# One more empty side step ahead of two products in a hybrid decoder trunk

## The chip, the cores and the metric

The kernel runs on one core of a Trainium2 chip. The metric is the device time of one execution in microseconds; the median of three runs of the kernel before is 1079.74 us (1079.16 to 1080.49). TensorE (PE in the profile) multiplies matrices, with its weight loads listed as PEld; VectorE (DVE), ScalarE (ACT) and GpSimd (POOL) do elementwise work; SyncE (SP) issues most transfers.

## What is computed

The input is 256 positions of width 2048. There are two layers. Layer 0 projects the normed input to six parts of 1024 and runs two token mixers side by side: HGRN2, a gated linear recurrence with 8 heads of 128, and Griffin RG-LRU, a linear recurrence over channels. Layer 1 is an mLSTM. Both end in an output projection and a gated embedding.

```
# HGRN2 (per head, chunks of 64)
q = silu(q_pre);  f = lb + (1 - lb) * sigmoid(f_pre);  k = (1 - lb) * sigmoid(-f_pre)
S_t = diag(f_t) S_{t-1} + k_t v_t^T;   o_t = S_t^T q_t
# RG-LRU
xc = causal_conv(xb)                                   # 4 taps
r = sigmoid(xc @ w_r + b_r);  ig = sigmoid(xc @ w_i + b_i)      # blocks of 128
a = exp(-8 r softplus(-lam));  u = sqrt(1 - a^2) * ig * xc
h_t = a_t h_{t-1} + u_t
# both: * silu(gate), then one output projection
```

All data are float32.

## The kernel before, in words

**Weights.** Each weight tile of 128 x 1024 comes by SyncE's queue into one of five raw buffers. ScalarE casts it to a high half (whi, line 123), VectorE subtracts to get a low half (wlo, line 124); there are four buffers of each, so the two tiles of one step and the two of the next. TensorE multiplies high by high and low activations (line 155) and low by high (line 162).

**Blocks and quarters.** A block (lines 147 to 175) is one output tile of 128 features over all 256 positions: 16 matmuls with high weights, then 16 with low ones. For the gates the tokens are on the partitions instead (project_tok, lines 193 to 213): an output tile of 512 columns is made in four quarters, each of two halves of 12 matmuls (lines 208 to 210).

**Side work.** The mixers are Python generators in lanes. The function pump (line 75) takes one step, up to the next yield, of the first generator of each lane. It is called once in each block, between the high and the low matmuls, and once in each quarter, between its two halves. A generator that ends lets the next one of its lane take its first step in the same call. The text calls these calls slots and numbers them from the first block after attention group 0 is started:

- slots 1 to 4: forget gates f of group 1 (f_proj); 5 to 8: its queries q (q_proj)
- slots 9 to 12 and 13 to 16: the two halves of the RG-LRU's input (xb_proj), each of four blocks; each two blocks are followed by a convolution (conv), one pass on ScalarE (line 705) and three instructions on VectorE (line 708) for each of two tiles
- slots 17 to 20 and 21 to 24: the four quarters of the two output gates of HGRN2 (gate_tok)

Attention of a group (lines 524 to 617) is eight steps: the product qf = q * f; five levels (block lengths 1, 2, 4, 8, 16), in each of which TensorE makes small products of k and qf (lines 541 and 546) and VectorE then updates qf (line 553), k (line 554) and the running products tot (line 556), and copies into C (lines 558 and 562); the blocks off the diagonal ("banks", lines 605 and 610, copied by ScalarE in lines 594, 614 and 615); and the read-out (lines 636 and 639) with its copies and squares on ScalarE (lines 640 and 643) and a Newton reciprocal root on VectorE (lines 216 to 222, 644 to 650). A half of the RG-LRU (lines 662 to 697) is five steps: the load of its gate weights; two gate products (line 674) with their sigmoids (line 678); tanh and exponential (lines 684 and 685) with a product (line 686) and a square (lines 690 and 691); and the root (line 693), a product (line 694) and the scan (line 696).

**Order on the engines.** Within an engine instructions run in the order that a list scheduler wrote down; the casts and subtractions of weights have a high priority, and side work of a slot is kept behind the last weight instruction issued before it. PSUM has three banks for side products (mx), three for blocks (mm) and two more (st).

Of the kernel before, what the change touches and what calls it, by code (L numbers as in the profile page):

```python
# [44 lines left out]
def trunk(ctx: ExitStack, tc: tile.TileContext, a, out):  # L45
# [58 lines left out]
    def pc(name, i=0, n=None):  # L104
        o, w = PRM[name]
        return prm[:, o + i:o + i + (n or 1)]
# [379 lines left out]
    with m0_scope:  # L486
# [37 lines left out]
        def attention(g):  # L524
# [2 lines left out]
            Ac = m0.tile([P, 4, P], F32, name="Ac", tag="Ac", bufs=1)  # L527
            C = m0.tile([P, 8, 32], F32, name="C", tag="C", bufs=1)
            qf = m0.tile([P, 1024], F32, name="qf", tag="qf", bufs=1)
            v.tensor_tensor(out=qf, in0=q, in1=f, op=ALU.mult)  # L530
            if g == 0:
                gp.memset(A, 0.0)
# [129 lines left out]
        def rg_lru(r, xc):  # L662
            bw = m0.tile([P, 2, 512], F32, name="bw", tag="bw", bufs=1)
            sy.dma_start(out=bw, in_=a["bw"][r])
            av = m0.tile([P, 1024], F32, name="av", tag="f")
            tt = m0.tile([P, 1024], F32, name="tt", tag="k")
            it = m0.tile([P, 1024], F32, name="it", tag="it", bufs=1)
            yield
            for j in range(2):
                for w, (dst, bias) in enumerate(((av, "bbr"), (it, "bbi"))):  # L670
                    ps = px.tile([P, 512], F32, name="mx", tag="mx")
                    for i in range(2):
                        c = 2 * j + i
                        te.matmul(ps[:, i * T:(i + 1) * T], bw[:, w, c * P:(c + 1) * P], xc[:, c * T:(c + 1) * T],
                                  start=True, stop=True)
                    for i in range(2):
                        c = 2 * j + i
                        s.activation(dst[:, c * T:(c + 1) * T], ps[:, i * T:(i + 1) * T], AF.Sigmoid,
                                     bias=pc(bias, 4 * r + c))
                yield  # L680
            for c in range(4):
                b = 4 * r + c
                cc = slice(c * T, (c + 1) * T)
                s.activation(tt[:, cc], av[:, cc], AF.Tanh, scale=sp8[:, b:b + 1])
                s.activation(av[:, cc], av[:, cc], AF.Exp, scale=spm8[:, b:b + 1])
            v.tensor_tensor(out=it, in0=it, in1=xc, op=ALU.mult)
            for j in range(2):
                sq = tp.tile([P, 512], F32, name="sq", tag="sq")
                jj = slice(j * 512, (j + 1) * 512)
                s.activation(sq, av[:, jj], AF.Square)  # L690
                v.scalar_tensor_tensor(tt[:, jj], sq, 1.0, tt[:, jj], op0=ALU.add, op1=ALU.mult)
            yield
            s.activation(tt, tt, AF.Sqrt, scale=0.25)
            v.tensor_tensor(out=it, in0=it, in1=tt, op=ALU.mult)
            v.memset(av.rearrange("p (c t) -> p c t", t=T)[:, :, 0:1], 0.0)
            v.tensor_tensor_scan(tt, av, it, 0.0, op0=ALU.mult, op1=ALU.add)
            res["h", r] = tt
# [16 lines left out]
        f_proj(0)  # L714
        q_proj(0)
        start("att", attention(0))
        f_proj(1)
        q_proj(1)
        start("att", attention(1))
        start("rg", rg_lru(0, xb_proj(0)))  # L720
        start("rg", rg_lru(1, xb_proj(1)))
        y = {}
        held = {}
# [487 lines left out]
```

## Time and profile before

| | |
|---|---|
| median of three runs | 1079.74 us |
| profiled execution | 1078.11 us |
| span of its instructions | 1076.3 us |
| mean granted TensorE clock | 0.997 |
| busy share PE, DVE, ACT, POOL | 98%, 68%, 54%, 6% |

The page gives busy time by engine and the groups of instructions that cost most. The view of waits lists which instruction stood idle until which other one ended: microseconds in total, times, the longest. The view by stage gives for a stretch of time: its length, busy time (and count) of TensorE, of its weight loads, of VectorE, ScalarE and GpSimd, the granted clock, the share of the DMA engines and GB/s. The view in order of time gives start and duration in microseconds, and in brackets the idle time before an instruction with what ended it; "x64" is a run of 64 instructions whose duration is that of the whole run. In these counts one multiplication in float32 appears as several passes.

### The profile page before, as it was taken

Reading aid. Unit: us, or ns where it says so; the run is one execution under the profiler, and the core shown is the slowest. Engines: PE = TensorE matmul, PEld = TensorE weight load, DVE = VectorE, ACT = ScalarE, POOL = GpSimd, SP = SyncE. Lnnn points to the kernel's source line nnn. Section 1 sums busy time; section 2 is a strip of 40 time slices with the busy share of each in tenths; the row PEclk is TensorE's granted clock in tenths of the full one; section 3 lists DMA queues with packets and bytes.
Section 4 is the critical chain, followed back from the end, with each engine's and each line's share of the span. In section 5 each row is a group of like instructions: output and inputs, shape, how many; then the busy total and the mean of one; then the engine's idle time right before and its main releaser. Section 6 shows DMA issues by size and latency. Waiting matters only on the chain.

```text
span 1076.3 us, 16798 instructions
## 1 busy us (share of the span) xinstructions
PE 1055.6 (98%) x6500; PEld 910.4 (85%) x6500; DVE 735.1 (68%) x1106; ACT 584.8 (54%) x863; POOL 67.8 (6%) x72
## 2 busy tenths in 40 slices
PE   7999999999999999999999999999999999999996
PEld 6888888887888888888888888888888888888886
DVE  6868978877767557777544887855456677555665
ACT  7565455688654435556444666654445554434543
POOL 0140400000000000112000000000000000000111
PEclk9999999999999999999999999999999999999998
DMA  9667444445655555555654655545555755555552
GB/s 337 166 230 217 153 160 149 154 138 194 240 195 193 193 186 188 185 189 194 195 193 158 216 188 167 176 157 195 195 195 190 247 184 181 196 192 176 181 176 79
DMA packets 56576, 201.76 MB, mean 187 GB/s; under 512 B 6472, under 2 KB 6864, under 8 KB 56496
## 3 DMA queue, kind: packets, MB, share of 16 engines
q1 hardware_dynamic: 54720, 195.04, 54.1%
q0 software_dynamic: 1776, 5.65, 1.8%
q8 instruction: 51, 0.84, 0.3%
q14 instruction: 29, 0.24, 0.1%
HBM read 198.55 MB, written 2.11 MB: 186 GB/s over the span
## 4 chain that ended last, share of the span: by engine, by line
PE 93%; DVE 2%; ACT 2%; issue 1%; DMA 1%; SPq 0%; DVEq 0%; ACTq 0%
PE mm L155 31%; PE mm L162 16%; PE mm L208 12%; PE mm L209 12%; PE mm L210 12%; DVE wlo L124 1%; PE mm L1065 1%; PE mm L1064 1%; PE mm L1063 1%; PE nu L899 1%; PE mx L546 1%; DMA raw<-in_pw_dram 1%; PE mx L428 0%; ACT whi L123 0%; PE mm L143 0%
## 5 line engine op out<-in xcount | busy, mean ns | idle before, releaser
L124 DVE TENSOR_TENSOR wlo<-raw,whi 128x1024 fp32r<-128x1024 f32 (+1 forms) x361 | 444.9, 1255 | 257.9 <-ACT whi L123 145.7
L123 ACT CAST whi<-raw 128x1024 fp32r<-128x1024 f32 (+1 forms) x361 | 377.5, 1048 | 333.9 <-PE mm L155 163.4
L155 PE MATMUL mm<-ahl,whi 128*128 128x512 f32 x1536 | 367.8, 391 | 0.0
L155 PEld LDWEIGHTS mm<-ahl,whi 128*128 128x128 f32 x1536 | 282.0, 188 | 55.7 <-DVE ahl L139 0.6
L208 PE MATMUL mm<-whi,ahl 128*128 128x512 f32 x608 | 238.7, 393 | 0.0
L210 PE MATMUL mm<-whi,ahl 128*128 128x512 f32 x608 | 236.7, 389 | 0.0
L209 PE MATMUL mm<-wlo,ahl 128*128 128x512 f32 x608 | 236.7, 389 | 0.0
L162 PE MATMUL mm<-ahl,wlo 128*128 128x256 f32 x1536 | 201.8, 284 | 0.0
L162 PEld LDWEIGHTS mm<-ahl,wlo 128*128 128x128 f32 x1536 | 195.7, 191 | 6.2
L210 PEld LDWEIGHTS mm<-whi,ahl 128*128 128x128 f32 x608 | 114.1, 188 | 24.0
L208 PEld LDWEIGHTS mm<-whi,ahl 128*128 128x128 f32 x608 | 114.2, 188 | 23.3
L209 PEld LDWEIGHTS mm<-wlo,ahl 128*128 128x128 f32 x608 | 114.2, 188 | 23.0
L179 ACT COPY sm<-mm 128x256 f32<-128x256 f32 x64 | 23.7, 371 | 43.8 <-PE mm L162 43.8
L180 DVE TENSOR_TENSOR mg<-mm,sm 128x256 f32<-128x256 f32 x64 | 26.6, 416 | 0.8 <-ACT sm L179 0.7
L772 DVE SCALAR_TENSOR_TENSOR qk<-mg,prm,qk 128x255 f32<-128x255 f32 (+2 forms) x48 | 21.5, 480 | 5.7 <-ACT qk L769 5.5
L261 POOL TENSOR_TENSOR acc<-acc,sq 128x512 f32<-128x512 f32 x6 | 9.7, 1621 | 193.8 <-ACT sq L260 193.8
L1051 POOL TENSOR_TENSOR pl<-pl,row 128x512 f32<-128x512 f32 x6 | 9.2, 1527 | 191.3 <-ACT sq L1035 191.3
L1063 PE MATMUL mm<-whi,ahl 128*128 128x256 f32 x64 | 18.3, 285 | 0.0
L1065 PE MATMUL mm<-whi,ahl 128*128 128x256 f32 x64 | 18.1, 283 | 0.0
L1064 PE MATMUL mm<-wlo,ahl 128*128 128x256 f32 x64 | 18.1, 283 | 0.0
L190 DVE TENSOR_TENSOR mg<-mg,hrs 128x512 f32<-128x512 f32 (+1 forms) x25 | 17.8, 714 | 0.3
L143 PE MATMUL mm<-ahl,whi 128*128 128x256 f32 x32 | 10.0, 314 | 7.4 <-ACT whi L123 7.4
(293 smaller groups left out, 772.1 us busy)
## 6 DMA issues: line engine op xcount, KB each, us to landing
raw<-in_ew_dram SPq DMA_DIRECT2D x64, 512.0 KB, 5.0
raw<-in_g_dram SPq DMA_DIRECT2D x56, 512.0 KB, 4.1
raw<-in_eo_dram SPq DMA_DIRECT2D x32, 512.0 KB, 4.7
raw<-in_ov_dram SPq DMA_DIRECT2D x32, 512.0 KB, 4.8
raw<-in_oqk_dram SPq DMA_DIRECT2D x32, 512.0 KB, 4.6
raw<-in_oog_dram SPq DMA_DIRECT2D x32, 512.0 KB, 4.5
raw<-in_oz_dram SPq DMA_DIRECT2D x32, 512.0 KB, 4.3
raw<-in_oo_dram SPq DMA_DIRECT2D x32, 512.0 KB, 4.1
```

The lines of the kernel that those rows point to most:

```text
L123: last["act"] = s.copy(h, r).ins
L124: last["dve"] = v.tensor_tensor(out=l, in0=r, in1=h.bitcast(F32), op=ALU.subtract).ins
L155: last["pe"] = te.matmul(ps, parts[k // 8][0][:, c:c + P], act[k // 2][2][:, (k % 2) * 512:(k % 2 + 1) * 512], start=(k == 0), stop=False).ins
L162: last["pe"] = te.matmul(ps[:, T:2 * T], parts[k // 8][1][:, c:c + P], act[k // 2][0][:, k % 2], start=False, stop=(k == KT - 1)).ins
L179: s.copy(small, ps[:, T:2 * T])
L180: v.tensor_tensor(out=dst, in0=ps[:, 0:T], in1=small, op=ALU.add)
L208: te.matmul(ps[hf], xh, wh, start=(k == 0), stop=False)
L209: te.matmul(ps[hf], xh, wl, start=False, stop=False)
L210: last["pe"] = te.matmul(ps[hf], xl, wh, start=False, stop=(k == KT - 1)).ins
L1063: te.matmul(ps[hf], xh, wh, start=(k == 0), stop=False)
L1064: te.matmul(ps[hf], xh, wl, start=False, stop=False)
L1065: last["pe"] = te.matmul(ps[hf], xl, wh, start=False, stop=(k == KT - 1)).ins
```

## The change

One yield is added in attention, ahead of the product qf, and one in rg_lru, ahead of the loop of gate products.

```
@@ -527,6 +527,7 @@
             Ac = m0.tile([P, 4, P], F32, name="Ac", tag="Ac", bufs=1)
             C = m0.tile([P, 8, 32], F32, name="C", tag="C", bufs=1)
             qf = m0.tile([P, 1024], F32, name="qf", tag="qf", bufs=1)
+            yield
             v.tensor_tensor(out=qf, in0=q, in1=f, op=ALU.mult)
             if g == 0:
                 gp.memset(A, 0.0)
@@ -665,6 +666,7 @@
             av = m0.tile([P, 1024], F32, name="av", tag="f")
             tt = m0.tile([P, 1024], F32, name="tt", tag="k")
             it = m0.tile([P, 1024], F32, name="it", tag="it", bufs=1)
             yield
+            yield
             for j in range(2):
                 for w, (dst, bias) in enumerate(((av, "bbr"), (it, "bbi"))):
```

No operation is added or removed by it. The slots of the steps are these:

| step | before | with the change |
|---|---|---|
| group 0: qf / levels / banks / read-out | 1 / 2-6 / 7 / 8 | 2 / 3-7 / 8 / 9 |
| group 1: qf / levels / banks / read-out | 9 / 10-14 / 15 / 16 | 10 / 11-15 / 16 / 17 |
| half 0: load / two gate products / exponential / root and scan | 13 / 14, 15 / 16 / 17 | 13 / 15, 16 / 17 / 18 |
| half 1: load / two gate products / exponential / root and scan | 17 / 18, 19 / 20 / 21 | 18 / 20, 21 / 22 / 23 |

Group 1's empty step shares slot 9 with the read-out of group 0. Half 1 is shifted by two slots, once through half 0 ahead of it in the lane. From the RG-LRU's gates (gate_mul) on the order of the engines is the same as before. ScalarE has 16 table loads in place of 15, since a tanh of the first output gate now stands between the root of half 0 and the sigmoids of half 1.

VectorE around the product qf of group 0, in slots 1 and 2; q and mg are the last query tile, tot the product of neighbouring forget gates. Before:

```order
L124 TENSOR_TENSOR wlo<-raw,whi 128x1024 x2
L180 TENSOR_TENSOR mg<-mm,sm 128x256
L556 TENSOR_TENSOR tot_1332<-f 128x512
L190 TENSOR_TENSOR mg<-mg,hrs 128x512
L517 SCALAR_TENSOR_TENSOR q<-mg,omb,th 128x256 x2
L530 TENSOR_TENSOR qf<-q,f 128x1024
```

With the change:

```order
L180 TENSOR_TENSOR mg<-mm,sm 128x256
L190 TENSOR_TENSOR mg<-mg,hrs 128x512
L517 SCALAR_TENSOR_TENSOR q<-mg,omb,th 128x256 x2
L531 TENSOR_TENSOR qf<-q,f 128x1024
L124 TENSOR_TENSOR wlo<-raw,whi 128x1024 x2
L180 TENSOR_TENSOR mg<-mm,sm 128x256
L557 TENSOR_TENSOR tot_1386<-f 128x512
```

The product qf stays directly behind q; tot moves behind it and behind a pair of low halves. On TensorE the level-1 products move behind the next block's high matmuls.

VectorE at the end of the last convolution (xc of half 1), in slots 16 to 18. Before:

```order
L708 SCALAR_TENSOR_TENSOR xc<-mg,prm,xc 128x253
L708 SCALAR_TENSOR_TENSOR xc<-mg,prm,xc 128x254
L696 SCALAR_TENSOR_TENSOR tt<-av,it 128x1024
L124 TENSOR_TENSOR wlo<-raw,whi 128x1024 x2
L708 SCALAR_TENSOR_TENSOR xc<-mg,prm,xc 128x253
```

With the change:

```order
L710 SCALAR_TENSOR_TENSOR xc<-mg,prm,xc 128x253
L710 SCALAR_TENSOR_TENSOR xc<-mg,prm,xc 128x254
L710 SCALAR_TENSOR_TENSOR xc<-mg,prm,xc 128x253
L124 TENSOR_TENSOR wlo<-raw,whi 128x1024 x2
L645 TENSOR_SCALAR hss<-hss 128x8
```

The conv's last instruction stood behind the scan of half 0 and the low halves of quarter four; now all six stand in a row ahead of the low halves of quarter three, and the read-out of group 1 (hss) follows.

ScalarE at the casts for quarters three and four and the next tile, in slots 17 to 20. Before:

```order
L693 ACT_TABLE_LOAD
L693 ACTIVATE tt<-tt 128x1024
L123 CAST whi<-raw 128x1024 x2
L705 ACTIVATE xc<-mg,prm 128x256 x2
L678 ACT_TABLE_LOAD
L678 ACTIVATE av<-mx,prm 128x256 x2
```

With the change:

```order
L641 COPY o<-mx 128x512
L644 ACTIVATE sq,hss<-mx 128x128 x2
L123 CAST whi<-raw 128x1024
L644 ACTIVATE sq,hss<-mx 128x128
L123 CAST whi<-raw 128x1024
L644 ACTIVATE sq,hss<-mx 128x128
L692 ACTIVATE sq<-av 128x512 x2
L695 ACT_TABLE_LOAD
L695 ACTIVATE tt<-tt 128x1024
L123 CAST whi<-raw 128x1024 x4
L444 ACT_TABLE_LOAD
```

The two casts for quarter three stood behind the root of half 0; they now stand among the read-out's squares, ahead of that root, and the casts for quarter four and the next tile's first quarter behind it. From half 0's first gate sigmoid to the second of the casts for quarter three ScalarE's list has, with the change, 8 sigmoids, 4 tanh, 4 exponentials, 3 table loads, 2 copies of blocks, 4 casts, 4 + 7 copies of attention blocks, 2 conv passes, 2 copies and 7 squares of the read-out. VectorE's list between the low halves of quarters three and four is two products for the square (line 691), the Newton steps, the scaling of the read-out (line 650) and the product of line 694.

More of the change, by code (lines that the diff above doesn't have):

```diff
@@ L529, in attention @@
             qf = m0.tile([P, 1024], F32, name="qf", tag="qf", bufs=1)
+            yield
             v.tensor_tensor(out=qf, in0=q, in1=f, op=ALU.mult)
@@ L667, in rg_lru @@
             it = m0.tile([P, 1024], F32, name="it", tag="it", bufs=1)
+            yield
             yield
```

## The prediction

> **What bounds the kernel now.** I read the first part of the page, then TensorE's waits, then busy time by stage, then the instructions in order of time where TensorE waits.
>
> ```profile
> PE 1055.6 (98%) x6500; PEld 910.4 (85%) x6500; DVE 735.1 (68%) x1106; ACT 584.8 (54%) x863; POOL 67.8 (6%) x72
> ```
>
> TensorE is busy for 1055.6 of 1076.3 us. A change that adds or removes no matmul can only act on the 20.7 us that are left. The view of waits, for TensorE alone, tells which instructions they belong to:
>
> ```profile
> PE mm L143 <- ACT whi L123: 7.4, 2, 6.1
> PE mx L674 <- DVE xc L708: 2.3, 1, 2.3
> PE mx L546 <- DVE qf L530: 1.9, 1, 1.9
> ```
>
> The first is the start of the kernel, out of reach. The other two lie in the two generators that are edited: a gate product waits for the convolved tile xc, and a level-1 product waits for qf, each once. After them comes a long stage with no idle time at all:
>
> ```profile
> 400.00:1040.00 640.00, 640.00 (x3252) 546.34 (x3252) 414.12 (x564) 331.42 (x470) 28.96 (x32) 1.00 0.57 189
> ```
>
> Busy is 640.00 of 640.00 us at a granted clock of 1.00, and the order of the engines there is that of before. So what TensorE wins or loses ahead of it arrives at the end undiminished; no later wait can eat it.
>
> **The change, part 1: the wait for qf.** TensorE in order of time (start, duration, what; idle before it in brackets), first group 0, then the same step of group 1:
>
> ```profile
> 119.14 0.84 PE L541 MATMUL mx<-q,k 128*32 128x32 f32 x64
> 121.86 0.73 PE L546 MATMUL mx<-qf,k 128*32 128x16 f32 x64 [1.88 <-DVE qf L530]
> 122.53 2.17 PE L162 MATMUL mm<-ahl,wlo 128*128 128x256 f32 x16
> ...
> 176.09 0.73 PE L541 MATMUL mx<-q,k 128*32 128x32 f32 x62
> ...
> 177.31 2.18 PE L162 MATMUL mm<-ahl,wlo 128*128 128x256 f32 x16
> ```
>
> The step takes 122.53 - 119.14 = 3.39 us in group 0 and 177.31 - 176.09 = 1.22 us in group 1. The wait therefore costs 2.17 us, a little more than the 1.88 in brackets. VectorE shows why qf is late:
>
> ```profile
> 113.57 1.44 DVE L556 TENSOR_TENSOR tot<-f 128x512 f32<-128x512 f32 x1
> ...
> 119.63 2.18 DVE L530 TENSOR_TENSOR qf<-q,f 128x1024 f32<-128x1024 f32 x1
> ...
> 171.45 1.23 DVE L530 TENSOR_TENSOR qf<-q,f 128x1024 f32<-128x1024 f32 x1
> ```
>
> ```profile
> 107.44 13.28 POOL L332 TENSOR_TENSOR pl<-pl,plrs 128x512 f32<-128x512 f32 x8 [5.88 <-DMA plrs<-plrsd]
> ```
>
> In group 0 the product takes 2.18 us beside POOL's eight products of 107.44 to 120.72, in group 1, with POOL idle, 1.23 us. It ends at 121.81, and TensorE starts at 121.86. With the change qf still stands right behind q on VectorE, and tot (1.44 us) moves from ahead of it to behind it, so qf ends at about 120.4. TensorE asks for it one block later: an unburdened block is about 5.6 us (the same start of side work in two neighbouring blocks), so at 119.14 + 5.6 = 124.8. That leaves 4.4 us of room; were qf no earlier, 3.0. **Gain 2.17 us**, and nothing is likely to give it back: qf would have to be later than any row of this stage shows.
>
> **Part 2: the wait for xc.** TensorE at the two gate products of the second RG-LRU half (slots 18 and 19), and VectorE's end of the convolution:
>
> ```profile
> 233.21 1.89 PE L674 MATMUL mx<-xc,bw 128*128 128x256 f32 x8
> 234.74 0.58 PE L208 MATMUL mm<-whi,ahl 128*128 128x512 f32 x1
> ...
> 240.40 1.02 PE L674 MATMUL mx<-xc,bw 128*128 128x256 f32 x4
> 243.73 1.13 PE L674 MATMUL mx<-xc,bw 128*128 128x256 f32 x4 [2.31 <-DVE xc L708]
> 244.51 0.58 PE L208 MATMUL mm<-whi,ahl 128*128 128x512 f32 x1
> ```
>
> ```profile
> 238.75 2.28 DVE L696 TENSOR_TENSOR_SCAN tt<-av,it 128x1024 f32<-128x1024 f32 x1
> ...
> 243.20 0.47 DVE L708 SCALAR_TENSOR_TENSOR xc<-mg,prm,xc 128x253 f32<-128x253 f32 x1
> ```
>
> Undisturbed the step takes 234.74 - 233.21 = 1.53 us, delayed 244.51 - 240.40 = 4.11: it costs 2.58 us. The last of the conv's instructions stands behind the first half's scan and a pair of low halves, since that half's end shares slot 17. With the change the end of the first half moves to slot 18, and all six conv instructions stand ahead of the weight pair. Counted from the end of the last conv block, that is ScalarE's conv pass at some 5 us (its backlog of that stage) and six instructions of 0.40 on VectorE, 8 us in all; TensorE asks for the tile only after a read-out (2.60) and seven half quarters (2.73 each; rows of both in (b)), 21.7 us. **Gain 2.58 us.**
>
> **Part 3: what is late next.** Three places come close. (a) A level of group 1 beside the conv of the first half. VectorE has one block to update qf and k between two levels:
>
> ```profile
> 189.50 0.74 PE L546 MATMUL mx<-qf,k 128*32 128x16 f32 x64
> ```
>
> ```profile
> 188.17 0.68 DVE L554 TENSOR_TENSOR k<-k,tot 128x512 f32<-128x512 f32 x1
> ```
>
> The k update ends at 188.85, 0.65 us ahead of TensorE. The level before it stands at this place now, and one conv instruction more (0.40 from start to start) lies between the two updates: 0.25 us of room. VectorE's own start there depends on ScalarE's conv pass, so I allow 0 to 0.7 us of loss and take 0.2.
>
> (b) The fourth quarter of the first output gate. The read-out of group 1 moves from slot 16 into slot 17, and with it ScalarE's copies and squares, ahead of the casts of weights. ScalarE ran the same list before from the first gate sigmoid on, with no wait behind its first row:
>
> ```profile
> 203.02 1.99 PE L674 MATMUL mx<-xc,bw 128*128 128x256 f32 x8
> ...
> 216.78 3.82 PE L155 MATMUL mm<-ahl,whi 128*128 128x512 f32 x16
> 220.43 1.05 PE L636 MATMUL mx<-vt,A 128*128 128x128 f32 x8
> ...
> 223.03 2.15 PE L162 MATMUL mm<-ahl,wlo 128*128 128x256 f32 x16
> 225.01 0.40 PE L208 MATMUL mm<-whi,ahl 128*128 128x512 f32 x1
> ```
>
> ```profile
> 204.19 0.84 ACT L678 ACTIVATE av<-mx,prm 128x256 f32<-128x256 f32 x2 [0.64 <-PE mx L674]
> ...
> 208.08 1.28 ACT L685 ACT_TABLE_LOAD   x1
> 209.38 0.51 ACT L685 ACTIVATE av<-av,spm 128x256 f32<-128x256 f32 x1
> 209.79 1.03 ACT L123 CAST whi<-raw 128x1024 fp32r<-128x1024 f32 x1
> ...
> 226.44 0.56 ACT L684 ACTIVATE tt<-av,sp 128x256 f32<-128x256 f32 x1
> ```
>
> The list takes 226.44 - 204.19 = 22.25 us. The new one, up to the second cast for quarter three, has a tanh and an exponential more (0.41 each from start to start) and a square less (about 0.25): 22.8 us, from 1.17 us behind the gate product (204.19 - 203.02). VectorE then makes that low half (1.2), ends the first half's and the read-out's arithmetic and makes the next low half:
>
> ```profile
> 228.75 0.69 DVE L691 SCALAR_TENSOR_TENSOR tt<-sq,tt 128x512 f32<-128x512 f32 x1 [0.34 <-ACT sq L690]
> ...
> 230.49 0.16 DVE L221 TENSOR_TENSOR hnt<-hnt,hny 128x8 f32<-128x8 f32 x1
> ...
> 231.89 0.17 DVE L222 SCALAR_TENSOR_TENSOR hnr<-hnt,hnr 128x8 f32<-128x8 f32 x1
> 231.97 1.22 DVE L694 TENSOR_TENSOR it<-it,tt 128x1024 f32<-128x1024 f32 x1
> 233.11 2.35 DVE L124 TENSOR_TENSOR wlo<-raw,whi 128x1024 fp32r<-128x1024 f32 x2
> ```
>
> That is two products of 0.6, nine Newton steps of 0.20 (seven from 230.49 to 231.89), two large products of 1.14, small ones of 0.6: 5.9 us; then 1.2 for the half. In all 1.17 + 22.8 + 1.2 + 5.9 + 1.2 = 32.3 us. TensorE in the same time: gate product to the end of the block after it 13.76 (203.02 to 216.78), read-out 2.60 (220.43 to 223.03), and six half quarters at 2.73 (three in 225.01 to 233.21), 16.4: 32.8 us, and 0.2 more to the first matmul that takes the low half. Room 0.7 us, so no loss. If instructions don't overlap as well as before (some 40, 0.06 us each) it is late by 1.7 us. I take 0.1; the range is 0 to 1.7.
>
> (c) The second gate product of slot 16 takes the PSUM bank that ScalarE's first three copies (L614) free; the spacing of the two is as before, so I book nothing.
>
> The page called ScalarE: Activation LUTs of the Trainium skill (section What ACT_TABLE_LOAD costs) gives about 1.28 us for a table load plus 1.38 us of drain, 2.66 us for each switch. The change adds one load, and by that rule ScalarE's three switches in (b) would take some 4.1 us more, TensorE would lose 3.4 us there, and the sum would be a gain of only about 1.2 us. The trace disagrees: from a load to the instruction behind it are 1.30 us (208.08 to 209.38), so this gets no chance beyond that of the moved wait below.
>
> Sum: 2.17 + 2.58 - 0.2 - 0.1 = 4.4 us. Against the profiled execution's own 1078.11 us (span 1076.3) that gives 1073.7; the median of the runs shown, 1079.74, lies 1.63 higher, and I carry the difference over: **1075.3 us**.
>
> **The rivals.** *Part of it comes back.* Places (a) and (b) take their worst, 0.7 + 1.7 = 2.4 us; the gain is 2.3, the time 1077.4. For it: ScalarE is busy 27.02 of 30 us from 220 to 250. Against it: the list ran without gaps before.
>
> ```profile
> 220.00:250.00 30.00, 27.70 (x143) 23.53 (x142) 21.19 (x39) 27.02 (x54) 0.00 (x0) 1.00 0.40 128
> ```
>
> *The wait only moves.* An empty step doesn't shorten what VectorE and ScalarE must do; the wait for xc turns into one of equal size for a low half in quarters two to four, and only the gain for qf, 2.2 us, less the 0.2 of (a), is left: 1077.7, no change that can be told (0.2%, 2.2 us, is about what a measurement tells from none). For it: the read-out and the half's end now meet in slots 17 and 18. Against it: xc was late through its place in VectorE's queue, not by total work; VectorE is busy only 21.19 of those 30 us.
>
> *Slower.* The low half of quarter four comes as late as the chain of before would bring it. Before, from the end of the list (226.44) to the end of the low pair ahead of the last conv instruction (243.20) lie 16.8 us. If that chain does not shorten, the pair is there 1.17 + 22.8 + 16.8 = 40.8 us behind the gate product, and TensorE wants its second half 32.8 + 1.6 = 34.4 us behind it: 6.4 us late, and with the 0.7 of (a) the loss is 7.1, the time 1079.74 + 2.4 = 1082.1. It decides for slower once that pair is more than 6.2 us late. Against it: those 16.8 us hold the scan, the conv and another pair (2.28 + 2.9 + 2.35), which stand elsewhere now. The Trainium skill's page TensorE: Matmul & The Clock Gate (Part 1) would add to such a wait a halved clock after some 3.4 us of idling; no run here shows it, the stages around both waits having a granted clock of 1.00.
>
> **How the numbers follow.** Forecast 0.62, part comes back 0.18, wait moves 0.13, slower 0.07. The forecast and the second are faster by over 0.2% (under 1077.6): 0.79 after the second's tail; within: 0.14; slower: 0.07. From below the range is bounded by the full gain, 4.75, and half a microsecond of spread of the median (runs lie 0.6 to 0.75 around it): 1074.3. From above it takes in the part that comes back and most of the moved wait: 1078.0.
>
> **What would show it.** TensorE's waits have neither qf nor xc; the level-1 step of group 0 takes about 1.2 us as in group 1, both gate products of the second half 1.5. The low half for the fourth quarter is ready within a microsecond of its first use. Wrong would be: a wait for wlo, for k or for a PSUM bank of over 2 us between 180 and 260 us, or a stage behind 400 us that has lost its full TensorE.

## The result and the profile after

The changed kernel took 1073.82 us (median of 6 runs, 1072.39 to 1075.84), the kernel before 1079.55 us (6 runs, 1077.04 to 1080.88). The ratio is 0.9946, with a 95% interval of 0.9934 to 0.9958: faster by 5.7 us where 4.4 were forecast, and half a microsecond below the low end of the range. The profiled execution took 1074.66 us, its span is 1072.9. One execution of the changed kernel (1169.53 us at a mean granted clock of 0.851, the profiled one of e4 below) and one of the kernel before (6046.13 us) are far out of line and left out of all that follows.

First the busy time by engine of the changed kernel (line numbers are one higher than before from 530 on, two higher from 669 on), then TensorE's waits:

```profile
PE 1056.5 (98%) x6500; PEld 911.6 (85%) x6500; DVE 735.0 (69%) x1106; ACT 585.8 (55%) x864; POOL 68.4 (6%) x72
```

```profile
PE mm L143 <- ACT whi L123: 6.8, 2, 6.3
PE mx L547 <- DVE k L555: 0.4, 1, 0.4
```

TensorE's busy time is nearly what it was (1055.6 before). The waits for qf and for xc are gone. A wait of 0.4 us for k is new. In order of time, TensorE at the level-1 step of group 0, at the new wait, and at the gate products of the second RG-LRU half:

```profile
125.52 0.73 PE L542 MATMUL mx<-q,k 128*32 128x32 f32 x62
...
126.74 1.46 PE L162 MATMUL mm<-ahl,wlo 128*128 128x256 f32 x10
...
145.81 0.73 PE L547 MATMUL mx<-qf,k 128*32 128x16 f32 x64 [0.40 <-DVE k L555]
...
243.24 1.89 PE L676 MATMUL mx<-xc,bw 128*128 128x256 f32 x8
244.78 0.58 PE L208 MATMUL mm<-whi,ahl 128*128 128x512 f32 x1
```

The level-1 step takes 126.74 - 125.52 = 1.22 us (3.39 before), the gate products 244.78 - 243.24 = 1.54 (4.11 before). VectorE's product qf is as slow as before, beside GpSimd's products of 108.34 to 122.17 us, but it ends at 121.03, 4.5 us ahead of this step:

```profile
118.82 2.21 DVE L531 TENSOR_TENSOR qf<-q,f 128x1024 f32<-128x1024 f32 x1
```

VectorE also shows where the new wait comes from:

```profile
141.46 0.73 DVE L507 TENSOR_SCALAR f<-f,omb,lb 128x256 f32<-128x256 f32 x2 [1.22 <-ACT f L503]
142.11 0.69 DVE L554 TENSOR_TENSOR qf<-qf,tot 128x512 f32<-128x512 f32 x1
142.71 2.35 DVE L124 TENSOR_TENSOR wlo<-raw,whi 128x1024 fp32r<-128x1024 f32 x2
144.98 0.68 DVE L555 TENSOR_TENSOR k<-k,tot 128x512 f32<-128x512 f32 x1
```

A level of group 0 now meets the forget gates f of group 1 (L507). VectorE waits 1.22 us for ScalarE there, and the update of k then stands behind a pair of low halves.

The stage from 400 to 1040 us has full TensorE as before:

```profile
400.00:1040.00 640.00, 640.00 (x3251) 546.37 (x3251) 414.69 (x564) 331.90 (x472) 28.97 (x32) 1.00 0.57 189
```

So the difference lies ahead of it. Two marks enclose the same work in both kernels: the first matmul of L155 behind 62 us, and the first transposes behind the output gates (L428). Before:

```profile
64.87 2.43 PE L155 MATMUL mm<-ahl,whi 128*128 128x512 f32 x10
...
266.51 1.03 PE L428 MATMUL mx<-cst,u 128*128 128x128 f32 x8
```

They are 201.64 us apart. In the changed kernel they are 263.07 - 65.69 = 197.38 us apart:

```profile
65.69 1.52 PE L155 MATMUL mm<-ahl,whi 128*128 128x512 f32 x6
...
263.07 1.03 PE L428 MATMUL mx<-cst,u 128*128 128x128 f32 x8
```

That is 4.26 us less, where the sum of the prediction was 4.4. From the second mark to the end of the span both take 809.8 us. What the forecast lacked is therefore not in this pair of profiles. The experiments look for it in other executions.

### The profile page after: what moved, and what is told of

Read it like the earlier page. It is cut to its first block, busy times and chain, and to the rows that moved or that the text cites. A ratio compares the mean times of both kernels' runs of the same rounds, so it can differ in the third digit from the quotient of the medians.

```text
span 1072.9 us, 16799 instructions
## 1 busy us (share of the span) xinstructions
PE 1056.5 (98%) x6500; PEld 911.6 (85%) x6500; DVE 735.0 (69%) x1106; ACT 585.8 (55%) x864; POOL 68.4 (6%) x72
## 4 chain that ended last, share of the span: by engine, by line
PE 98%; DVE 1%; DMA 0%; ACT 0%; SPq 0%; issue 0%; DVEq 0%
PE mm L155 32%; PE mm L162 17%; PE mm L208 13%; PE mm L210 13%; PE mm L209 13%; PE mm L1067 1%; PE mm L1066 1%; PE mm L1065 1%; PE mx L676 1%; PE nu L901 1%; PE mx L547 1%; DMA raw<-in_pw_dram 0%; PE mx L428 0%; PE mm L143 0%; PE mm L145 0%; PE mm L144 0%
## 5 line engine op out<-in xcount | busy, mean ns | idle before, releaser
L155 PE MATMUL mm<-ahl,whi 128*128 128x512 f32 x1536 | 367.8, 391 | 0.0
L155 PEld LDWEIGHTS mm<-ahl,whi 128*128 128x128 f32 x1536 | 282.0, 188 | 55.7 <-DVE ahl L139 0.6
L180 DVE TENSOR_TENSOR mg<-mm,sm 128x256 f32<-128x256 f32 x64 | 26.7, 417 | 0.4 <-ACT sm L179 0.3
```

What stands on the lines that cost most here:

```text
L155: last["pe"] = te.matmul(ps, parts[k // 8][0][:, c:c + P], act[k // 2][2][:, (k % 2) * 512:(k % 2 + 1) * 512], start=(k == 0), stop=False).ins
L180: v.tensor_tensor(out=dst, in0=ps[:, 0:T], in1=small, op=ALU.add)
```

## The experiments

**The same kernel again, and each empty step alone.** e1 is the kernel before, e4 the changed kernel, both without an edit. e2 and e3 have one of the two steps each:

```diff
             qf = m0.tile([P, 1024], F32, name="qf", tag="qf", bufs=1)
+            yield                                  # e2 only
             v.tensor_tensor(out=qf, in0=q, in1=f, op=ALU.mult)
...
             it = m0.tile([P, 1024], F32, name="it", tag="it", bufs=1)
             yield
+            yield                                  # e3 only
             for j in range(2):
```

> The kernel before once more, unchanged, against itself: what two timings of one and the same kernel differ by. Theory S (the runs of one kernel scatter by 3 to 4 us, because the start, up to the first projection, differs from run to run): the ratio is 1.000 within 0.2%, single runs lie 3 us or more apart, and the point in the profile at which the first block of f of group 1 begins moves by up to 1 us against the earlier profile while everything from there to the end keeps its length. Rival (runs repeat within 0.1%): the runs lie within 1.1 us and the start is at the same place.

> Only the empty step ahead of qf. Theory Q (xc is late by its place in VectorE's queue behind the scan; with the attention one slot later its order puts all six conv instructions ahead of the scan, though half 0 and half 1 keep their slots): both waits go, 4.75 less 0.4 for the level in slot 5, ratio about 0.996. Rival (each empty step removes its own wait alone): the wait for xc stays at some 2.6 us, the gain is 2.17 - 0.4 = 1.8 us, ratio 0.9984.

> Only the empty step ahead of the gate products. Both theories: the wait for xc goes (2.58 us), the wait for qf stays at 1.9 us in the list, ratio about 0.9976; no wait of 0.4 us in slot 5, since the levels stand where they stood. Rival of the prediction (the wait only moves to low halves of the output gates' quarters): no gain, and a wait for wlo of 1 to 2.6 us between 225 and 260 us.

> The changed kernel once more, unchanged, on the same chip. Theory S (the body of the kernel wins the 4.75 us of the two waits less one new wait of 0.4, so 4.3 us, and the 5.7 us of the first timing hold 1.4 us of scatter): ratio about 0.9960, 4.0 to 4.8 us, and from slot 1 to the end its profile is 4.3 us shorter than that of the kernel before. Rival L (there is a gain that the two waits don't show, for example fewer waits too short to be listed): ratio 0.9947 again, and the profile from slot 1 to the end is 5.5 us or more shorter.

Measured: e1 1079.58 us (ratio 1.0005, interval 0.9995 to 1.0015), e4 1074.58 over its four other executions (0.9956, 0.9943 to 0.9969; no profile of it is used), e2 1074.81 (0.9955, 0.9944 to 0.9967), e3 1077.13 (0.9974, 0.9964 to 0.9984). TensorE's waits, e2 and then e3:

```profile
PE mm L143 <- ACT whi L123: 6.8, 2, 5.3
PE mx L547 <- DVE k L555: 1.0, 2, 0.8
```

```profile
PE mm L143 <- ACT whi L123: 6.3, 2, 6.1
PE mx L546 <- DVE qf L530: 1.6, 1, 1.6
PE mx L675 <- ACT A L614: 0.5, 1, 0.5
```

The step ahead of qf alone removes both waits and has the time of the changed kernel. It moves the rest of attention by one slot, the read-outs included, while the RG-LRU keeps its slots. On VectorE all six conv instructions of the second half then stand ahead of the first half's scan, as e2 shows:

```profile
228.67 2.45 DVE L709 SCALAR_TENSOR_TENSOR xc<-mg,prm,xc 128x255 f32<-128x255 f32 x6
...
232.17 2.29 DVE L697 TENSOR_TENSOR_SCAN tt<-av,it 128x1024 f32<-128x1024 f32 x1
```

Either step is thus enough to remove the wait for xc. The step ahead of the gate products alone removes the wait for xc and brings a wait of 0.5 us for the PSUM bank of place (c). e1 showed something that neither of its theories had. It waits for xc as long as the kernel before did, yet its marks are 203.21 us apart (64.15 to 267.36), 1.57 more. TensorE behind that wait in e1:

```profile
239.63 1.02 PE L674 MATMUL mx<-xc,bw 128*128 128x256 f32 x4
242.98 2.08 PE L674 MATMUL mx<-xc,bw 128*128 128x256 f32 x4 [2.33 <-DVE xc L708]
244.50 0.99 PE L208 MATMUL mm<-whi,ahl 128*128 128x512 f32 x1
245.28 0.63 PE L209 MATMUL mm<-wlo,ahl 128*128 128x512 f32 x1
...
246.90 0.39 PE L208 MATMUL mm<-whi,ahl 128*128 128x512 f32 x1
```

The four gate matmuls take 2.08 us where the prediction's row has 1.13, and the next ones start 0.42 to 0.78 us apart, where later ones have 0.23. From here on theory C stood against rival N: a wait of some 2 us brings TensorE's clock down behind it, or the clock has nothing to do with it.

**The wait for qf, its cause and the new wait for k.** e6 was to hold GpSimd's last products back, e11 leaves seven of the eight out (the PLE norm's factor is then missing there), e7 puts the updates of a level ahead of the pairs of low halves in the changed kernel:

```diff
         rs = free_copy(rt, "plrs")                            # e6
         yield
+        for _ in range(28):
+            yield
         for j, pl in enumerate(pls):
             x3 = pl.rearrange("p (j t) -> p j t", j=2)
-            gp.tensor_tensor(out=x3, in0=x3, ...)             # e11
+            if j == 7:
+                gp.tensor_tensor(out=x3, in0=x3, ...)
...
+                with tc.high_priority(offset=400):            # e7, on the changed kernel
                     v.tensor_tensor(out=qv, in0=qv, ...)
                     v.tensor_tensor(out=kv, in0=kv, ...)
```

> The kernel before, with GpSimd's eight last products (L332) 28 side steps later, so that they no longer run beside VectorE's q, tot and qf of group 0; nothing else moves. Theory S (qf is late because VectorE's operations run at half pace beside GpSimd): the low pair falls from 4.19 to about 2.35 us, qf from 2.18 to 1.23, the wait of 1.88 us for qf is gone, the wait of 2.3 us for xc stays: about 1077.4 (1079.5 less 2.2). Rival O (the order alone makes it late: tot stands ahead of qf and q waits for ScalarE): qf is still asked for too early and the wait stays at 1 us or more: 1078.5 to 1079.5. VectorE's operations beside the moved products get slower there; should TensorE wait for one of them, the gain is smaller.

> The kernel before without seven of GpSimd's eight last products in the PLE norm (L332; the norm's factor is left out there, so the values of that part are not the reference's). In e6 they stayed where they were, since nothing on GpSimd stood in between. Theory S (qf is late because VectorE runs at half pace beside them): low pair 2.35 us in place of 4.19, q and qf 0.88 and 1.23 in place of 2.18 each, qf ready before TensorE asks for it at about 120, no wait for qf, the wait for xc stays; about 2.2 us less than before, 1077.4, and up to 0.5 less where a lowered clock behind that wait goes too. Rival O (the order alone): a wait for qf of 1 us or more stays: 1078.5 or more.

> The changed kernel, with the updates of qf and k between two levels (L554, L555) raised in priority, so that the k update of slot 5 stands ahead of the pair of low halves on VectorE. If the new wait of 0.40 us for k costs what its bracket shows, it is gone and the time is that of the changed kernel less 0.4 us: about 1073.9 where that one has 1074.3. Rival: the low pair, now behind the update (0.7 us), is late for its block, and the time is the same or up to 0.5 us more.

e6 missed its aim: the products ran at 106.92 us as ever, since a step that issues nothing does not hold back an engine with nothing else to do. It took 1079.98 us and serves as the kernel before once more. e11 took 1076.31 us (0.9979, 0.9968 to 0.9990). VectorE in the kernel before, then VectorE and TensorE in e11:

```profile
109.12 4.19 DVE L124 TENSOR_TENSOR wlo<-raw,whi 128x1024 fp32r<-128x1024 f32 x2 [2.93 <-issue]
```

```profile
109.47 2.36 DVE L124 TENSOR_TENSOR wlo<-raw,whi 128x1024 fp32r<-128x1024 f32 x2 [2.93 <-issue]
...
112.08 0.68 DVE L557 TENSOR_TENSOR tot<-f 128x512 f32<-128x512 f32 x1
...
114.99 1.23 DVE L531 TENSOR_TENSOR qf<-q,f 128x1024 f32<-128x1024 f32 x1
```

```profile
119.49 0.73 PE L542 MATMUL mx<-q,k 128*32 128x32 f32 x62
...
120.70 2.18 PE L162 MATMUL mm<-ahl,wlo 128*128 128x256 f32 x16
```

The order is that of before, with tot ahead of qf, and qf is ready at 116.2, 3.8 us before TensorE wants it. Rival O falls: in the old order the wait for qf came from GpSimd's products beside VectorE. Its marks are 199.52 us apart, 2.12 less than before, for the 2.17 of the prediction's first term. e7 took 1073.21 us (0.9938, 0.9926 to 0.9951), and the wait for k is gone from its profile.

**The wait for xc made longer and shorter.** e8 does the first half's scan twice, e10 does so with both scans ahead of the last conv instruction, e9 scans half of the elements (the recurrence of two of the four blocks of that half is left out):

```diff
             v.tensor_tensor_scan(tt, av, it, 0.0, op0=ALU.mult, op1=ALU.add)
+            if r == 0:                                                   # e8
+                v.tensor_tensor_scan(tt, av, it, 0.0, op0=ALU.mult, op1=ALU.add)
...
+            with tc.high_priority(offset=20 if r == 0 else 0):           # e10: both scans in here
...
+            n = 512 if r == 0 else 1024                                  # e9
+            v.tensor_tensor_scan(tt[:, 0:n], av[:, 0:n], it[:, 0:n], 0.0, ...)
```

> The kernel before, with the first RG-LRU half's scan (2.28 us on VectorE) done twice with the same result. The last conv instruction for xc stands behind it, so the wait for xc grows from 2.3 to about 4.6 us. Theory C (a wait of this length brings down the granted clock of TensorE behind it in some executions, and a longer one does so always): the profile shows a granted clock below 1.00 in the stretch behind the wait and doubled matmul times for some us; the median rises by the 2.28 us and 1 to 2.5 us more, 1083 to 1084.5. Rival N (the clock has nothing to do with the wait; the executions differ for other reasons): plus 2.28 us alone, 1081.8, mean clock as in the kernel before.

> The kernel before, with the first RG-LRU half's scan done twice (same result), and this time both scans in front of the last conv instruction for xc (in e8 the second scan stood behind it and the wait kept its 2.3 us). The wait for xc grows to about 4.5 us. Theory C (TensorE's granted clock falls behind a wait of some 2 us in many executions, and behind a longer one in all): matmuls of 0.4 to 0.6 us spacing in place of 0.23 behind it for 2 to 4 us, granted clock well below 1.00 there, median 2.2 us for the scan and 0 to 1.5 us more: 1082 to 1083.5. Rival N (the lowered clock comes at that place for another reason, not for the wait): the same lowered stretch as in e1, plus 2.2 us, 1081.8, and the profile would show it no longer and no deeper than in e1.

> The kernel before, with the first RG-LRU half's scan over 512 of its 1024 elements only (the recurrence of two of its four channel blocks is left out, so the values of that half are not the reference's). The scan is 1.14 us shorter and the wait for xc falls to about 1.2 us. Theory C: no lowered clock behind it in the profile, the mean clock of the runs is 0.997 to 0.998 where the kernel before has 0.996, and the median falls by 1.14 us and 1 to 1.6 us more: 1076.8 to 1077.4. Rival N: 1.14 us alone, 1078.4, mean clock unchanged.

In e8 the second scan went behind the last conv instruction, so the wait stayed 2.3 us and the time 1079.87 (1.0002, 0.9992 to 1.0012): again the kernel before once more. e10 took 1081.01 (1.0014, 1.0003 to 1.0025), less than both theories said, since five matmuls of the next product slipped in front of the wait, which grew to 3.46 us and not to 4.5. e9 took 1077.60 (0.9983, 0.9973 to 0.9994); its wait fell to 1.76, not to 1.2. The median fell by 2.1 (1.8 by the ratio), more than the 0.6 by which the step got shorter (3.54 us in place of 4.11). That leans to C, but the interval holds N's 1.1 as well. The profiled execution of e9 shows a lowered clock at the other wait, that for qf, for which neither theory said anything in this run. In a table of stretches (busy time of TensorE first, granted clock third from the end), e1, e9, e10 and the kernel before:

```profile
239.45:242.86 3.41, 1.20 (x6) 0.71 (x4) 3.41 (x4) 2.53 (x5) 0.00 (x0) 1.00 0.12 30
242.86:246.27 3.41, 3.29 (x8) 2.65 (x9) 0.07 (x1) 2.65 (x4) 0.00 (x0) 0.50 0.69 237
246.27:249.69 3.42, 3.42 (x17) 2.82 (x16) 1.37 (x2) 2.59 (x4) 0.00 (x0) 1.00 0.10 41
...
1072.30:1075.71 3.41, 0.00 (x0) 0.00 (x0) 0.00 (x0) 0.00 (x0) 0.00 (x0) 0.50 0.85 308
```

```profile
119.18:122.59 3.41, 1.53 (x87) 1.02 (x88) 3.38 (x3) 1.87 (x2) 3.41 (x3) 1.00 0.00 0
122.59:126.01 3.42, 3.42 (x76) 3.38 (x68) 3.42 (x4) 0.00 (x0) 0.90 (x1) 0.50 0.15 22
...
242.06:245.47 3.41, 1.65 (x9) 1.12 (x8) 2.52 (x3) 3.36 (x7) 0.00 (x0) 1.00 0.35 124
245.47:248.89 3.42, 3.42 (x17) 2.83 (x16) 0.11 (x1) 2.92 (x4) 0.00 (x0) 1.00 0.53 182
```

```profile
118.27:121.68 3.41, 1.61 (x68) 1.05 (x66) 3.38 (x3) 2.11 (x3) 3.41 (x3) 1.00 0.00 0
121.68:125.09 3.41, 3.33 (x75) 3.30 (x76) 3.41 (x4) 0.00 (x0) 1.15 (x1) 0.50 0.09 14
...
244.55:247.97 3.42, 0.68 (x3) 0.62 (x4) 2.65 (x3) 0.84 (x2) 0.00 (x0) 1.00 0.73 255
247.97:251.38 3.41, 3.41 (x10) 2.66 (x9) 1.09 (x1) 1.42 (x2) 0.00 (x0) 0.50 0.05 20
```

```profile
239.80:243.21 3.41, 1.62 (x8) 1.05 (x6) 3.41 (x4) 2.13 (x5) 0.00 (x0) 1.00 0.04 10
243.21:246.63 3.42, 2.90 (x13) 2.46 (x14) 0.46 (x2) 3.38 (x5) 0.00 (x0) 1.00 0.71 247
```

Every lowered stretch ahead of the end of the kernel is 3.41 us long at a granted clock of exactly 0.50. In one execution they lie on one grid: in e10 they start at 121.68 and 247.97, 126.29 apart, which is 37 times 3.413; in e1 at 242.86 and, at the end, 1072.30, 829.44 apart or 243 times 3.413. So the grid of any execution can be laid from the lowered stretch at its end, and that is how the windows above were cut for the executions or places without one. What decides is TensorE's idle time in the window before:

| Execution, wait | Idle of 3.41 us (less busy time) | Granted clock in the next window |
|---|---|---|
| e10, xc | 2.74 | 0.50 |
| e6, e13, xc | 2.30 | 0.50 |
| e1, e8, xc | 2.21 | 0.50 |
| e9, qf | 1.88 | 0.50 |
| e10, qf | 1.80 | 0.50 |
| before, xc | 1.79 | 1.00 |
| e9, xc | 1.76 | 1.00 |
| e11, xc | 1.56 | 1.00 |
| e6, e13, qf | 1.47 | 1.00 |

The windows around the waits for qf that the table leaves out (before, e1, e8, e3, e16) hold 1.53 us or less, and none is followed by a lowered one. The end of the kernel, where TensorE runs out of work, gives one more reading in each of the 17 profiles: the window ahead of the last lowered stretch holds 2.0 us of idle time or more, the one ahead of that 1.56 or less.

Rival N falls: the lowered clock follows the wait, at both places, and only where one window holds about 1.8 us of it. Whether it does depends on where the grid lies, which changes from execution to execution.

**Two steps in place of one, and the changed kernel again.** e5 is the kernel before with two empty steps at each place, e12 is the changed kernel:

```diff
+            yield
+            yield
             v.tensor_tensor(out=qf, in0=q, in1=f, op=ALU.mult)     # and the same ahead of the gate products
```

> Two empty steps at each of the two places in place of one. If the one step already takes all that these waits hold, the time is that of the changed kernel (about 1074.2) as long as nothing new is late. By the prediction's places (a) and (b) every further step leaves less room there, 0.15 and 0.2 us in the profile of the changed kernel, so a new wait of 0.3 to 2 us for a level's k or for a low half of the output gate is the rival: 1074.5 to 1076.5.

> The changed kernel once more. Theory C: with no wait over half a microsecond behind the start, no stretch from 66 to 1040 us has a granted clock under 1.00, and the executions lie closer together than those of the kernel before; median 1073.8 to 1074.7. Rival N: lowered stretches show up in the same places as in the kernel before (120 to 130 us, 242 to 250 us).

e5 took 1074.75 us (0.9955, 0.9942 to 0.9967), no better than one step; the wait for k is gone and another has come, for a PSUM bank that the output gate's accumulation (L445) frees:

```profile
249.75 0.51 PE L208 MATMUL mm<-whi,ahl 128*128 128x512 f32 x1 [0.75 <-DVE u L445]
```

e12 took 1075.06 us (0.9960, 0.9948 to 0.9972), 0.4 above what C said, with a granted clock of 1.00 from 66 to 1040 us.

**A last set, on what was open.** e13 is the kernel before, e14 the changed one, e15 the kernel of e7 and e16 that of e3:

> The kernel before once more. Theory C: behind the wait for xc (2.3 us) or the wait for qf (1.9 us) the granted clock is under 1.00 in more executions than not, so a lowered stretch shows at 242 to 250 us (about 1.6 us lost) or at 120 to 130 us (about 1.5 us lost) with some two chances in three, and most of the executions have a mean clock of 0.996 or less. Rival N: none here, mean clocks as in the changed kernel (0.997 to 0.998).

> The changed kernel once more, as partner for e15 and e13 in one call. Theory C: median 1074 to 1075, mean clocks 0.997 to 0.998 throughout, the wait of 0.4 to 0.5 us for k in the profile.

> The kernel of e7 (level updates of qf and k ahead of the pairs of low halves) beside the changed kernel in one call. If the wait for k costs what its bracket shows, 0.4 to 0.5 us under e14; if the 1.4 us between e7 and the changed kernel's other sets came from the edit, 1 us or more under it; if from the sets, equal within 0.5 us.

> The kernel of e3 (the empty step ahead of the gate products alone) for another profiled execution. Sum: the wait for xc (2.58 us) and the lowered clock behind it go, a wait of 0.5 us for a PSUM bank comes, the wait for qf (1.9 us) stays, with a lowered clock behind it in one execution of three: 1076.5 to 1077.5. Its spread lies ahead of the first product of the stage (before 66 us) if start-up makes it, or at 120 to 130 us if the clock does.

Measured: e13 1079.45 us (0.9999, 0.9989 to 1.0008), e14 1074.67 (0.9953, 0.9941 to 0.9965), e15 1073.23 (0.9942, 0.9929 to 0.9954), e16 1075.08 (0.9962, 0.9950 to 0.9974). e13 has a lowered stretch behind xc (243.99 to 247.40), as C said. The waits of e14 show that the new wait for k is not always as small as in the first profile:

```profile
PE mm L143 <- ACT whi L123: 6.2, 2, 5.1
PE mx L547 <- DVE k L555: 1.4, 2, 0.8
```

e15 lies 1.44 us under e14, and e7 had the same time as e15, while the sets of the changed kernel lie at 1073.82, 1074.58, 1075.06 and 1074.67. The version with the level updates ahead has the lowest times here, but the intervals of its ratio and e14's still overlap. Its marks say more: they are 196.91 and 196.85 us apart, against 197.38, 197.56 and 198.47 in the changed kernel. e16 lies 1.4 us below the low end of its sum and 2.05 below e3, which is the same kernel. Its marks are 199.85 apart and e3's 199.50; of the 1.46 us between these two profiled executions, 1.11 lie ahead of the first mark (65.17 against 64.06). So start-up makes most of that spread, not the clock. Why most of e3's executions lay above 1076 at a mean clock of 0.997 to 0.998 stays open, since its profile is of the fastest one.

How often the clock falls can be counted without a profile, as each execution has a mean granted clock. In the 17 profiled executions it was 0.994 to 0.996 in the six with a lowered stretch ahead of the end, and 0.997 or 0.998 in the eleven without. Of 87 executions of the kernel before that ran beside the experiments, 63 had 0.996 or less (mean time 1079.76 us), 24 had more (1078.75). Of the 20 of the changed kernel none had. With one wait left it was 2 of 12 (e11), 3 of 12 (e9, where the shortened xc wait no longer reaches 1.8 us) and none of 13 (e3 and e16).

## Why the prediction was right, and where it was wrong

*What bounds the kernel now.* Right: all of the gain arose ahead of 266 us and arrived at the end.

*Part 1, 2.17 us.* Right in cause and size. The level-1 step fell to 1.22 us, since TensorE asks for qf one block later, and with GpSimd's products left out, in the old order, 2.12 us were gained. Wrong was "nothing is likely to give it back": qf was safe, but k was not. In slot 5 the update of k for group 0 falls behind the forget gates of group 1, a place that the prediction did not look at. It costs 0.4, 0.5 and 1.4 us of waiting in the three profiles of the changed kernel.

*Part 2, 2.58 us.* Right for the execution that it was read from (the step fell from 4.11 to 1.54), and too small for the kernel. Its reason, that the end of the first half shares slot 17, is not the whole of it: in e2 that end stays in slot 17 and the wait is gone all the same, so the two terms of the sum do not belong to one step each. Why the list scheduler then puts the conv ahead of the scan is not shown. It priced the wait by its length in one profile, and said of a halved clock that no run here showed it. With a lowered stretch behind it the kernel takes 1.6 us more (e1), and by their mean clock 63 of 87 executions had such a stretch at one wait or the other. In the profile that lay at hand the wait fell 1.79 us into one window and 0.52 into the next, so nothing showed.

*Part 3.* (a) and (b) cost nothing, closer than thought. In (a) the k update ends 0.15 us ahead of TensorE, in (b) the first low half of the pair is ready some 0.2 us before quarter four takes it. The update, and then the pair:

```profile
186.90 0.68 DVE L555 TENSOR_TENSOR k<-k,f 128x512 f32<-128x512 f32 x1
```

```profile
239.34 2.35 DVE L124 TENSOR_TENSOR wlo<-raw,whi 128x1024 fp32r<-128x1024 f32 x2
```

The 0.3 us that were booked for them about fit the wait for k in its better case, which is luck: it stands at another place. (c) cost nothing in the changed kernel and 0.5 us with the RG-LRU step alone. The Trainium skill's 2.66 us for a table switch (ScalarE: Activation LUTs, section What ACT_TABLE_LOAD costs) did not come true: in the changed kernel the instruction behind the load starts 1.29 to 1.30 us after it at each of the three switches of (b), and TensorE waited for nothing there.

*The step that failed* is the last line of the sum: "the median of the runs shown, 1079.74, lies 1.63 higher, and I carry the difference over". By that line the time is the changed kernel's profile, 1073.7, plus 1.63. The profile came out at 1074.66, later by 1.0, of which 0.82 is a longer start-up (first mark at 65.69 against 64.87). The term of 1.63 came out at -0.84 in the six runs of the result (1073.82 less 1074.66) and at 0.0 over all 20 executions (median 1074.67). It was sized at 1.63 where it measured nothing or less, and the longer start-up hid a part of that.

The difference is no constant of the kernel. Of the 1.63, 0.25 is the three runs shown lying above the 87 executions (median 1079.49). Another 0.74 lies between that median and the mean of the executions whose clock did not fall (1078.75), and 0.64 between these and the one profile. The middle piece is the lowered clock, and the change takes its cause away. The outer pieces are how a set of three and a single profile happened to fall, and so is the result's set, 0.85 below the median of the 20; their cause stays open.

The marks say the same of the clock. In the five profiled executions of the kernel before and its like (before, e1, e6, e8, e13) they are 202.64 us apart on average, in the three of the changed kernel 197.80. Of these 4.84, 4.26 stand in the first pair of profiles. The rest, 0.6, is what the lowered clock adds to the kernel before (1.0 with its at times shorter waits for qf) less what the longer waits for k take from the changed kernel (0.4). The medians of all executions, 1079.49 (87) and 1074.67 (20), differ by 4.82. So close an agreement is partly luck: the start-up ahead of the marks took 0.83 us more in these three profiles than in those five, so the whole profiled executions differ by only 4.02.

*The range* ended at 1074.3, from "the full gain, 4.75, and half a microsecond of spread"; these words give 1079.74 - 4.75 - 0.5 = 1074.5. Over four sets the changed kernel's median lay between 1073.82 and 1075.06, and the sets of e3 and e16, one kernel, lay 2.05 us apart. Half a microsecond was too little for that. The result's set is the lowest of its four; over all executions the time is inside the range, and the forecast of 1075.3 was 0.6 us too high.

*The rivals.* None came about. "Part of it comes back" names the right kind of event, a wait for k, but at another place and at 0.4 to 1.4 us in place of 2.4. The remark that no run showed a halved clock held for the one profile at hand; e1 showed it behind the same wait.

## What to carry to other kernels

Where TensorE waits for more than 1.8 us in a kernel that otherwise keeps it full, look at more than one profiled execution, and price the wait at its length plus half a window (1.7 us at most; 1.57 in e1) times the share of executions whose mean clock is down. Cutting such a wait below the limit already wins the second part, as e9's shortened wait for xc shows. When steps are moved by one slot, list every tile that now meets another producer in VectorE's queue, not only the tile whose wait was to go, and do not carry the gap between a profile and a median from one kernel to the next. Here a median of five to eight runs could be off by 1 to 2 us (e3 and e16).

## What the runs showed of the hardware

TensorE's granted clock is decided in windows of 3.41 us on a grid that runs through the whole execution. At the two waits, in twelve readings, a window with 1.80 us or more of idle time was followed by one at 0.50, a window with 1.79 or less was not. Edges are good to some 0.05 us, so the limit is known as about 1.8 us and no closer. The Trainium skill (TensorE: Matmul & The Clock Gate, Part 1) states the length, 3413 ns, and that the window is free-running; both agree. It puts the fall of the clock behind an idle window; here half an idle window was enough. As an estimate from these figures: were every place of the grid equally likely, a wait of 2.32 us would leave 1.8 us in one window in (2.32 - 0.19) / 3.41 = 62% of executions. The kernel before had 72% (63 of 87) with two waits, e11 only 2 of 12 with its one wait of 2.31, so the grid is not evenly spread against the program; what fixes it stays open.

VectorE's operations with two inputs from SBUF ran at about half their pace beside GpSimd's products: the pair of low halves took 4.19 us and 2.36 without them, qf 2.18 and 1.23. The addition of L180, which reads one input from PSUM, took 0.41 and 0.42. The time to the first block of L155 varies by itself, from 64.06 to 65.81 us over the 17 profiled executions; why is not shown.
